# Two groups by seven products in more pairs of a trunk's weight chunks, and the squares of x in two turns

## The chip, the core and the metric

The kernel runs on one core of one Trainium2 chip. The metric is device time of one execution in microseconds (us); the median of three runs is quoted, and the profile is of one execution of its own. The engines are TensorE (PE; PEld is its weight load), VectorE (DVE), ScalarE (ACT), GpSimd (POOL) and SyncE (SP), which here only issues transfers. SPq and POOLq are the queues of SP and POOL.

## What is computed

Two layers of a trunk on x of 256 rows by 2048 columns, in float32. Cut to what matters:

```python
for i in range(2):
    h = rmsnorm(x, norm_mix_g[i])
    glu_in, q, k, v, f_logit, g_conv, g_attn = split(h @ w_in[i])
    y_conv = conformer_conv(glu_in, ...)          # depthwise conv over 31 rows, LayerNorm, swish, @ w_conv_out
    y_attn = forgetting_attention(q, k, v, log_sigmoid(f_logit + b)) @ w_attn_out[i]      # 8 heads of 128
    x = x + (sigmoid(g_conv) * y_conv + sigmoid(g_attn) * y_attn) @ w_out[i]
    gate, up = split(rmsnorm(x, norm_ffn_g[i]) @ w_gate_up[i])                           # 2 x 5632 columns
    x = x + (silu(gate) * up) @ w_down[i]
    x = x + sigmoid(rmsnorm(x, norm_ple_g[i]) @ w_ple_gate[i]) * (p[i] @ w_ple_proj[i])
return rmsnorm(x, final_g)
```

## The kernel before

**Three products for one.** Every weight matrix is read in chunks of 512 output columns, and a chunk in groups of four K tiles of 128 rows (a transfer brings two K tiles, 128x1024). TensorE works on float32r values, so each weight tile is split: `split` (L143, L144) makes a high part `wh` with a copy on ACT and a low part `wl` with a subtraction on DVE; the activations are split in the same way. `Sum.add` (L186 to L188) issues high x high, high x low and low x high, each a matmul of 512 columns. A plain group of two chunks is 4 K tiles x 2 chunks x 2 blocks of 128 rows x 3 = 48 matmuls.

**Seven products.** `fast_chunks` takes a pair of chunks, `w1` and `w2`, and treats the first groups by the seven products of the Strassen-Winograd scheme: two chunks and two halves of the K tiles make a 2x2 block product. Such a group is 7 x 2 K tiles x 3 = 42 matmuls. It needs seven splits where a plain group needs four, and combinations of the raw weights: POOL issues one transfer that adds onto a loaded tile (L278), DVE adds and subtracts (L273, L274; the helpers `add` and `sub` are also used for the sums at the end, from PSUM). The activations' side, eight blocks, is made once per norm group by `Fast` (L360, L366, L375, L376); `Norm(..., fast=n)` makes it for the first n groups of four K tiles. The argument `fast` of `fast_chunks` is the list of these, and `ks` are the first K tiles of the plain groups.

**What sets the order.** A scheduler puts the instructions of each engine in an order, mostly that of the code; every engine then works through its own in that order. Buffers bound how far an engine runs ahead: eight of `raw`, five of `wh` and five of `wl`, four single PSUM banks (`ms`) and two double ones (`mm`). Work beside the products is handed out in steps: `run()` calls the functions that wait in `turns` and one of `tasks` (the attention heads: scores and softmax, transposes, product with v; twelve tasks for four heads); `fill(n)` gives n units of credit to `background`, DVE's depthwise conv and the conv branch's norm. `chunk` does one `run()` and one `fill(7)` for each of its groups. In `fast_chunks` `go()` treats half a plain group; those that are called among the seven products are quiet, the later ones do a `run()` and a `fill` of 3 or 4. What is left is flushed: `while tasks: run()` behind the attention branch's gates, `while background: fill(9)` behind the first pair of the conv branch's gates.

**The stages of a layer, in order:** GLU input, values, keys and queries by `chunk`; the attention branch's gates in two pairs (`sigmoids(GATE_B, 1)` and `sigmoids(GATE_B + 2, 1)`, one group by seven products each); the attention projection in four chunks; the conv branch's gates in two pairs of two groups each, with the conv projection; `wOut`; then gate-and-up in parts of 3, 4 and 4 column chunks, c = 0 to 10, where a pair is the gate chunk and the up chunk of one c, each part followed by two down pairs; then the embeddings' gate in two pairs (n = 0 and 2) with one group each. Pair c = 0 is plain. The others take `FAST[c % 2]` groups: two for even c, one for odd c.

**The beginning of the first layer.** x is read twice, transposed for the first chunk and in rows (`xt`) for the residual and the sums of squares. `late(b)` issues the two halves of `xt` in two turns, each released by a tiny ACT copy (L532, L533); its third turn loads the remaining vectors (L536, L537), takes the squares of all of x (`squares`, L424, eight ACT instructions), finishes the norm and hands over to `early`, which builds the `Fast` blocks.

Of the kernel before, what the change touches and what calls it, by code (L numbers as in the profile page):

```python
# [16 lines left out]
P = 128  # L17
# [11 lines left out]
KD = D // P  # L29
# [5 lines left out]
PAIRS = 28  # L35
WARM = 14
RAWS = 8

FAST = (2, 1)
CONV = 7  # L40
PAUSE = 2 * CONV, lambda: None

# [5 lines left out]
def trunk(ctx, tc, xT, xR, pT, wI, wF, wC, wA, wOut, wGU, wD, wPG, wPP, vec, bF, gF, out):  # L48
    nc = tc.nc
# [31 lines left out]
    turns = deque()  # L81
# [400 lines left out]
    norm = Norm(0)  # L482
# [46 lines left out]
    def late(b):  # L529

        if b < 2:
            act.activation(xt[:, b, :1], recent[0][:, 0, :1], AF.Copy)  # L532
            nc.sync.dma_start(xt[:, b, :], xR[:, b, :])  # L533
            turns.append(lambda: late(b + 1))
            return
        nc.sync.dma_start(vecs[:, KD:], vec[:, KD:])  # L536
        nc.sync.dma_start(bfs, bF.rearrange("l h -> (l h)").partition_broadcast(P))  # L537
        for n in range(N4):
            norm.squares(n)
        norm.finish()  # L540
        turns.append(early)

    for i in range(L):
# [296 lines left out]
        def sigmoids(c, nf):  # L840

            ts = []

            def gate(t):
                for b in range(2):
                    act.activation(t[:, b, :], t[:, b, :], AF.Sigmoid, scale=norm.r(b))  # L846
                ts.append(t)

            gate(fast_chunks(norm.fast[:nf], wI[i, c], wI[i, c + 1], norm.xs, range(4 * nf, KD, 4), gate))
            return ts  # L850
# [1 line left out]
        def gated_by(t, pp):  # L852
            dve.tensor_tensor(t, t, pp, op=ALU.mult)

        y_att = sigmoids(GATE_B, 1) + sigmoids(GATE_B + 2, 1)
        while tasks:
            run()
        for n in range(N4):
# [19 lines left out]
            xc = xt[:, :, n * 512 : (n + 1) * 512]  # L878
            dve.tensor_tensor(xc, xc, acc, op=ALU.add)

        norm = Norm(g_ffn, fast=max(FAST))
        def onto_x(norm, n):
            def go(y):
                residual(n, y)
# [11 lines left out]
            )  # L896


        after = Norm(g_ple, fast=1)
        c0 = 0  # L900
        for part, nch in enumerate(FFN_PARTS):
            hid = {}
            fast_hid = [Fast() for _ in range(nch - 2)]
            for c in range(c0, c0 + nch):
                w1, w2 = wGU[i, 2 * c], wGU[i, 2 * c + 1]
                o = pair() if c == 0 else None

                def gate(g):
                    nonlocal o
                    if o is None:  # L910
                        o = g
                    for b in range(2):
                        act.activation(o[:, b, :], g[:, b, :], AF.Silu, scale=norm.r(b))

                if c == 0:
                    gate(chunk(by_four(w1), norm.xs))
                    up = chunk(by_four(w2), norm.xs)
                else:
                    nf = FAST[c % len(FAST)]
                    up = fast_chunks(norm.fast[:nf], w1, w2, norm.xs, range(4 * nf, KD, 4), gate)  # L920
                for b in range(2):
                    dve.scalar_tensor_tensor(
                        o[:, b, :], up[:, b, :], norm.r(b), o[:, b, :], op0=ALU.mult, op1=ALU.mult
                    )
                turns.append(
                    lambda c=c, o=o, hid=hid, fast=fast_hid[c - c0] if c - c0 < len(fast_hid) else None:
                    operand(hid, 4 * c, lambda b: o[:, b, :], fast)
                )
# [63 lines left out]
        for n in range(0, N4, 2):  # L992
            for m in range(2):
                e.append(pair())
                for b, t in enumerate(chunk([(wPP[i, n + m], range(2))], ps)):
                    act.activation(e[n + m][:, b, :], t, AF.Copy)
            ending = last and n == N4 - 2
            y = fast_chunks(
                norm.fast, wPG[i, n], wPG[i, n + 1], norm.xs, (4, 8, 12), embedded(n),
                by_block=end if ending else None,  # L1000
            )
            if not ending:
                embedded(n + 1)(y)
# [61 lines left out]
```

## Time and profile before

| | |
|---|---|
| median of three runs | 2809.96 us (2809.64 to 2810.13) |
| the profiled execution's own time | 2809.66 us |
| its span in the profile | 2808.0 us |
| granted TensorE clock, mean | 0.999 |
| transfers | 578.96 MB, mean 206 GB/s |

In a row of the costliest groups the columns are line, engine, operation, what it writes and reads (buffer numbers left out), shapes and count; then busy time, mean of one in ns, and the idle time of the engine ahead of it with what ended it. A timeline row is start, length, engine, line, operation, tiles, count, and in brackets idle time and its releaser. The ends of matmuls are modelled, so their rate is read from their starts.

### The profile page before, as it was taken

The page shows a single profiled execution, that of the slowest core. Times are in us where ns is not written, and L with a number is a line of the kernel's source. Part 1 is how long each engine was busy: PE and PEld are TensorE (multiplying, and loading weights), DVE is VectorE, ACT ScalarE, POOL GpSimd, SP SyncE. Part 2 cuts the span into 40 slices and gives each one's busy share as a digit, 9 for nine tenths or more (in the row PEclk, how much of TensorE's full clock was granted, in tenths as well). Part 3 has the DMA queues.
Part 4 walks back from the last instruction along what each step waited for, and adds up shares of the span by engine and source line. Part 5 has one row for each costly group of instructions (what it writes and reads, how often), then busy time and mean ns, then how long its engine had stood idle before and what let it go on. Part 6 is the DMA issues. An engine that isn't in the chain of part 4 may idle for free.

```text
span 2808.0 us, 34895 instructions
## 1 busy us (share of the span) xinstructions
PE 2789.8 (99%) x12640; PEld 2307.2 (82%) x12640; DVE 2429.0 (87%) x2927; ACT 1628.9 (58%) x1962; POOL 68.7 (2%) x109
## 2 busy tenths in 40 slices
PE   9999999999999999999999999999999999999998
PEld 7888888888888888888888888888888888888886
DVE  7998788887989888889869987888789899888897
ACT  7445655565556555656644456555655465555565
POOL 0000000000000000000000000000000000000000
PEclk9999999999999999999999999999999999999999
DMA  8555467665677666676655555666666676676673
GB/s 298 188 184 184 168 191 224 204 214 189 216 226 227 202 224 219 216 222 215 203 173 191 185 168 173 220 213 190 228 192 213 217 230 220 203 233 210 211 247 121
DMA packets 159870, 578.96 MB, mean 206 GB/s; under 512 B 18001, under 2 KB 18257, under 8 KB 159441
## 3 DMA queue, kind: packets, MB, share of 16 engines
q1 hardware_dynamic: 149040, 539.50, 56.0%
q0 software_dynamic: 9792, 35.66, 7.2%
q8 instruction: 99, 1.62, 0.2%
q10 hardware_dynamic: 864, 1.57, 0.2%
q14 instruction: 75, 0.61, 0.1%
HBM read 574.56 MB, written 2.10 MB: 205 GB/s over the span
## 4 chain that ended last, share of the span: by engine, by line
PE 95%; DVE 1%; ACT 1%; DMA 1%; issue 1%; SPq 0%; POOL 0%; POOLq 0%; ACTq 0%
PE mm L186 26%; PE mm L187 26%; PE mm L188 26%; PE ms L186 5%; PE ms L188 5%; PE ms L187 5%; PE ms L336 2%; DMA raw<-in_wI_dram 1%; ACT wh L143 1%; DVE wl L144 1%; PE ms L724 0%; DVE raw L273 0%; PE ms L753 0%; PE ms L743 0%; ACT pair L846 0%
## 5 line engine op out<-in xcount | busy, mean ns | idle before, releaser
L143 ACT ACTIVATE wh<-raw 128x1024 fp32r<-128x1024 f32 x1218 | 1271.2, 1059 | 1057.3 <-PE mm L188 669.6
L144 DVE TENSOR_TENSOR wl<-raw,wh 128x1024 fp32r<-128x1024 f32 x1218 | 1463.9, 1221 | 295.1 <-ACT wh L143 288.2
L186 PE MATMUL mm<-wh,pair 128*128 128x512 f32 x3340 | 1307.7, 392 | 0.7 <-ACT pair L326 0.3
L187 PE MATMUL mm<-wl,pair 128*128 128x512 f32 x3340 | 1301.9, 390 | 1.4 <-DVE wl L144 1.4
L188 PE MATMUL mm<-wh,pair 128*128 128x512 f32 x3340 | 1302.1, 390 | 0.5 <-DVE pair L327 0.5
L188 PEld LDWEIGHTS mm<-wh,pair 128*128 128x128 f32 x3340 | 627.0, 188 | 132.4 <-DVE pair L327 1.3
L187 PEld LDWEIGHTS mm<-wl,pair 128*128 128x128 f32 x3340 | 627.4, 188 | 130.6 <-DVE wl L144 3.0
L186 PEld LDWEIGHTS mm<-wh,pair 128*128 128x128 f32 x3340 | 627.3, 188 | 129.5 <-ACT wh L143 1.5
L186 PE MATMUL ms<-wh,pair 128*128 128x512 f32 x588 | 229.5, 391 | 1.9 <-ACT wh L143 1.9
L188 PE MATMUL ms<-wh,pair 128*128 128x512 f32 x588 | 228.9, 389 | 0.0
L187 PE MATMUL ms<-wl,pair 128*128 128x512 f32 x588 | 228.9, 389 | 0.0
L567 DVE SCALAR_TENSOR_TENSOR pair<-pair,vecs,pair 128x256 f32<-128x256 f32 x480 | 201.8, 480 | 0.0
L273 DVE TENSOR_TENSOR raw<-raw,raw 128x1024 f32<-128x1024 f32 x136 | 166.2, 1222 | 2.3
L186 PEld LDWEIGHTS ms<-wh,pair 128*128 128x128 f32 x588 | 110.4, 188 | 27.2 <-ACT wh L143 3.3
L188 PEld LDWEIGHTS ms<-wh,pair 128*128 128x128 f32 x588 | 110.4, 188 | 23.0
L187 PEld LDWEIGHTS ms<-wl,pair 128*128 128x128 f32 x588 | 110.4, 188 | 22.3
L273 DVE TENSOR_TENSOR pair<-pair,ms 128x512 f32<-128x512 f32 x144 | 94.0, 680 | 0.0
L274 DVE TENSOR_TENSOR raw<-raw,raw 128x1024 f32<-128x1024 f32 x68 | 83.3, 1225 | 2.3
L274 DVE TENSOR_TENSOR pair<-mm,pair 128x1024 f32<-128x1024 f32 (+1 forms) x48 | 58.2, 1212 | 18.1 <-PE mm L188 18.1
L273 DVE TENSOR_TENSOR pair<-pair,mm 128x1024 f32<-128x1024 f32 x48 | 58.4, 1216 | 8.6 <-PE mm L188 8.6
L376 DVE TENSOR_TENSOR pair<-pair,pair 128x1024 fp32r<-128x1024 f32 x48 | 58.1, 1219 | 0.0
L375 ACT ACTIVATE pair<-pair 128x1024 fp32r<-128x1024 f32 x48 | 50.2, 1056 | 2.1 <-DVE pair L366 1.2
(167 smaller groups left out, 1054.7 us busy)
## 6 DMA issues: line engine op xcount, KB each, us to landing
raw<-in_wGU_dram SPq DMA_DIRECT2D x352, 512.0 KB, 4.9
raw<-in_wI_dram SPq DMA_DIRECT2D x287, 512.0 KB, 4.0
raw<-in_wD_dram SPq DMA_DIRECT2D x176, 512.0 KB, 5.0
raw<-in_wOut_dram SPq DMA_DIRECT2D x64, 512.0 KB, 4.9
raw<-in_wPG_dram SPq DMA_DIRECT2D x64, 512.0 KB, 5.0
raw<-in_wA_dram SPq DMA_DIRECT2D x32, 512.0 KB, 4.4
raw<-in_wC_dram SPq DMA_DIRECT2D x32, 512.0 KB, 5.6
raw<-in_wGU_dram POOLq DMA_DIRECT2D x30, 512.0 KB, 8.0
```

Of the source, the lines that this page charges most:

```text
L143: act.activation(h, raw, AF.Copy)
L144: dve.tensor_tensor(l, raw, h.bitcast(F32), op=ALU.subtract)
L186: pe.matmul(self.t, lhsT=xh, rhs=wh, start=start, stop=False)
L187: pe.matmul(self.t, lhsT=xh, rhs=wl, start=False, stop=False)
L188: pe.matmul(self.t, lhsT=xl, rhs=wh, start=False, stop=self.left == 0)
L273: add = lambda o, a, b: dve.tensor_tensor(o, a, b, op=ALU.add)
L274: sub = lambda o, a, b: dve.tensor_tensor(o, a, b, op=ALU.subtract)
L336: pe.transpose(pt[:, kk * S + b * P : kk * S + (b + 1) * P], src(b)[:, c : c + P], ident)
L375: act.activation(h, t, AF.Copy)
L376: dve.tensor_tensor(l, t, h.bitcast(F32), op=ALU.subtract)
L567: dve.scalar_tensor_tensor(cv[c], u[c][:, j : j + S], w, cv[c], op0=ALU.mult, op1=ALU.add,)
```

## The change

```diff
-FAST = (2, 1)
...
-        nc.sync.dma_start(vecs[:, KD:], vec[:, KD:])
-        nc.sync.dma_start(bfs, bF.rearrange("l h -> (l h)").partition_broadcast(P))
+        if b == 2:
+            nc.sync.dma_start(vecs[:, KD:], vec[:, KD:])
+            nc.sync.dma_start(bfs, bF.rearrange("l h -> (l h)").partition_broadcast(P))
         for n in range(N4):
-            norm.squares(n)
+            norm.squares(n, [b - 2])
+        if b == 2:
+            turns.append(lambda: late(3))
+            return
         norm.finish()
         turns.append(early)
...
-        y_att = sigmoids(GATE_B, 1) + sigmoids(GATE_B + 2, 1)
+        y_att = sigmoids(GATE_B, 2) + sigmoids(GATE_B + 2, 2)
...
-        norm = Norm(g_ffn, fast=max(FAST))
+        norm = Norm(g_ffn, fast=2)
...
-        after = Norm(g_ple, fast=1)
+        after = Norm(g_ple, fast=2)
...
-                    nf = FAST[c % len(FAST)]
+                    nf = 1 if c == c0 else 2
...
-                norm.fast, wPG[i, n], wPG[i, n + 1], norm.xs, (4, 8, 12), embedded(n),
+                norm.fast[: 1 + n // 2], wPG[i, n], wPG[i, n + 1], norm.xs, range(4 + 2 * n, KD, 4), embedded(n),
```

In gate-and-up all pairs but the first of a part have two groups by seven products (c = 1, 5 and 9 had one; c0 is the first c of a part: 0, 3, 7). Both pairs of the attention branch's gates have two instead of one, and so has the embeddings' second pair, for which the norm ahead of it now makes two `Fast` groups. The squares of x are taken in two turns, one for each block of 128 rows, and `early` comes a turn later. Line numbers in the new file are two lower up to the diff's first place in `late` and two higher behind it: L144 is L142, L274 is L272, L735 is L737.

In gate-and-up, DVE's rows at pair 5 of the first layer, from the last split of its first group on, before (`raw` and `wl` are weight tiles, `pair` with `ms` the sums from PSUM):

```order
L144 TENSOR_TENSOR wl_7531<-raw_7423,wh_7530 128x1024
L274 TENSOR_TENSOR pair_7414<-pair_7414,ms_7510 128x512
L144 TENSOR_TENSOR wl_7548<-raw_7545,wh_7547 128x1024
L273 TENSOR_TENSOR pair_7415<-pair_7414,ms_7498 128x512
L144 TENSOR_TENSOR wl_7592<-raw_7589,wh_7591 128x1024
L273 TENSOR_TENSOR pair_7414<-pair_7414,ms_7522 128x512
L273 TENSOR_TENSOR pair_7415<-pair_7415,ms_7522 128x512
L144 TENSOR_TENSOR wl_7610<-raw_7607,wh_7609 128x1024
```

and at the end of the second group of the same pair now:

```order
L142 TENSOR_TENSOR wl_7646<-raw_7572,wh_7645 128x1024
L271 TENSOR_TENSOR raw_7572<-raw_7572,raw_7575 128x1024
L272 TENSOR_TENSOR raw_7570<-raw_7572,raw_7570 128x1024
L142 TENSOR_TENSOR wl_7657<-raw_7572,wh_7656 128x1024
L271 TENSOR_TENSOR raw_7577<-raw_7577,raw_7572 128x1024
L142 TENSOR_TENSOR wl_7668<-raw_7570,wh_7667 128x1024
L142 TENSOR_TENSOR wl_7679<-raw_7577,wh_7678 128x1024
L142 TENSOR_TENSOR wl_7699<-raw_7696,wh_7698 128x1024
L272 TENSOR_TENSOR pair_7444<-pair_7444,ms_7540 128x512
L142 TENSOR_TENSOR wl_7743<-raw_7740,wh_7742 128x1024
```

The sums from PSUM (`ms`) stood directly behind the first group; a second group with its combinations of raw weights now stands ahead of them.

At the end of the attention branch's gates, TensorE's rows before, at the product with v (L753, L754) of one of the layer's last heads, with the first of the twelve weight products behind it:

```order
L753 MATMUL ms_2937<-tmp_2869,pair_1371 128x256
L754 MATMUL ms_2937<-tmp_2869,pair_1371 128x128
L186 MATMUL mm_2719<-wh_2948,pair_494 128x512
L187 MATMUL mm_2719<-wl_2949,pair_494 128x512
L188 MATMUL mm_2719<-wh_2948,pair_495 128x512
```

and now, with a head's product with v (L755, L756), the transposes of the next (L745) and the scores of the one behind it (L726, L728, L729) in one row:

```order
L755 MATMUL ms_2991<-tmp_2924,pair_1371 128x256
L756 MATMUL ms_2991<-tmp_2924,pair_1371 128x128
L745 MATMUL ms_3000<-ident,tmp_2949 128x128
L726 MATMUL ms_3007<-pair_2027,pair_2491 128x128
L728 MATMUL ms_3007<-chs_922,nident 128x128
L745 MATMUL ms_3000<-ident,tmp_2949 128x128 x2
L729 MATMUL ms_3007<-chs_922,nident 128x128
L726 MATMUL ms_3017<-pair_2027,pair_2491 128x256
L728 MATMUL ms_3017<-chs_922,nident 128x256
L729 MATMUL ms_3017<-chs_922,nident 128x256
L755 MATMUL ms_3027<-tmp_3004,pair_1371 128x256
L756 MATMUL ms_3027<-tmp_3004,pair_1371 128x128
```

The tasks that were spread among the second pair's products are left for the flush behind it and stand closer together; 26, 10, 19 and 17 weight products lie between the scores and the transposes of the last four heads.

At the beginning, SP's rows with the second half of `xt`, before:

```order
L137 DMA raw_377<-in_wI_dram 128x1024
L533 DMA xt<-in_xR_dram 128x2048
L536 DMA vecs<-in_vec_dram 128x624
L537 DMA bfs<-in_bF_dram 128x16
L137 DMA raw_430<-in_wI_dram 128x1024
```

and now:

```order
L135 DMA raw_377<-in_wI_dram 128x1024
L535 DMA vecs<-in_vec_dram 128x624
L531 DMA xt<-in_xR_dram 128x2048
L536 DMA bfs<-in_bF_dram 128x16
L135 DMA raw_417<-in_wI_dram 128x1024
```

The load of `xt` waits for the tiny ACT copy, which stood ahead of the copy of the first GLU chunk out of PSUM (L595) and now stands behind it; the weight loads behind it on SP wait with it.

## The prediction

> **What bounds the kernel now.** I read the page first: busy time by engine, then the chain that ended last, then the costliest groups.
>
> ```profile
> PE 2789.8 (99%) x12640; PEld 2307.2 (82%) x12640; DVE 2429.0 (87%) x2927; ACT 1628.9 (58%) x1962; POOL 68.7 (2%) x109
> ...
> PE 95%; DVE 1%; ACT 1%; DMA 1%; issue 1%; SPq 0%; POOL 0%; POOLq 0%; ACTq 0%
> ...
> L143 ACT ACTIVATE wh<-raw 128x1024 fp32r<-128x1024 f32 x1218 | 1271.2, 1059 | 1057.3 <-PE mm L188 669.6
> L144 DVE TENSOR_TENSOR wl<-raw,wh 128x1024 fp32r<-128x1024 f32 x1218 | 1463.9, 1221 | 295.1 <-ACT wh L143 288.2
> ...
> L273 DVE TENSOR_TENSOR raw<-raw,raw 128x1024 f32<-128x1024 f32 x136 | 166.2, 1222 | 2.3
> ```
>
> 95% of the chain is TensorE, and ACT's largest wait (669.6 us) is for TensorE to give a buffer back: the copies run ahead until the five buffers of `wh` are full. That alone would make each matmul left out a gain. But DVE is at 87% of the whole and must make a low part for every weight tile, so the second question is where DVE is short. The timelines of DVE and TensorE around pair 5 of the first layer's gate-and-up loop (one group by seven products, between two pairs that have two) give the pace of both.
>
> ```profile
> 872.67 1.22 DVE L144 TENSOR_TENSOR wl<-raw,wh 128x1024 fp32r<-128x1024 f32 x1
> ...
> 880.28 0.39 PE L187 MATMUL ms<-wl,pair 128*128 128x512 f32 x1
> ...
> 893.40 1.22 DVE L144 TENSOR_TENSOR wl<-raw,wh 128x1024 fp32r<-128x1024 f32 x1
> ...
> 895.01 0.39 PE L186 MATMUL mm<-wh,pair 128*128 128x512 f32 x1
> 895.24 0.39 PE L187 MATMUL mm<-wl,pair 128*128 128x512 f32 x1
> ...
> 897.51 0.40 PE L188 MATMUL mm<-wh,pair 128*128 128x512 f32 x1
> ...
> 852.80 4.62 DVE L144 TENSOR_TENSOR wl<-raw,wh 128x1024 fp32r<-128x1024 f32 x4
> ```
>
> The twelve products from 895.01 to 897.51 start (897.51 - 895.01) / 11 = 0.227 us apart: although each row says 0.39, they overlap and nothing waits. On DVE four splits take 4.62 us, so they start (4.62 - 1.22) / 3 = 1.13 us apart. The low part made from 872.67 to 873.89 is used at 880.28: DVE leads by 6.39 us when this pair begins. The one made from 893.40 to 894.62 is used at 895.24: the lead has sunk to 0.62 us at the end of the group by seven products, because such a group wants ten DVE instructions for 9.5 us of products. **The lead is what can be spent**; below zero TensorE idles.
>
> **The products saved.** The sums by window are cut at the first product of the pairs 4, 5, 6 and of the first down pair behind them (columns: length, then busy time and count of PE, PEld, DVE, ACT, POOL; the clock; DMA share; GB/s).
>
> ```profile
> 838.33:880.05 41.72, 41.72 (x189) 34.62 (x188) 41.23 (x42) 27.42 (x29) 0.86 (x1) 1.00 0.65 209
> 880.05:923.14 43.09, 43.09 (x195) 35.74 (x194) 36.18 (x37) 24.30 (x26) 1.70 (x2) 1.00 0.71 219
> 923.14:964.87 41.73, 41.73 (x190) 34.62 (x188) 39.76 (x38) 25.52 (x27) 0.85 (x1) 1.00 0.70 226
> 964.87:1007.96 43.09, 43.09 (x196) 35.74 (x195) 34.35 (x33) 21.20 (x22) 1.70 (x2) 1.00 0.71 218
> ```
>
> A pair with one group takes 43.09, with two 41.73: a converted group is worth 1.36 us, which is six products of 0.227 (48 become 42). Per layer the change converts three groups in gate-and-up (pairs 1, 5, 9), two in the attention branch's gates (one in each pair) and one in the embeddings' second pair; 6 in a layer, 12 in all: 12 x 1.36 = **-16.4 us**, 72 products. The order of instructions has exactly 72 products fewer, so that the change might not do what it says is excluded.
>
> **What each converted group adds.** Three more splits (L143 and L144) and three combinations (two at L273, one at L274), which last as long as a split (1222 ns beside 1221): six DVE instructions, 6 x 1.13 = 6.8 us of DVE; 3.2 us of ACT, which is 58% busy and waits for TensorE most; and one more accumulating transfer on POOL's queue (SP issues four loads either way).
>
> ```profile
> raw<-in_wGU_dram SPq DMA_DIRECT2D x352, 512.0 KB, 4.9
> ...
> raw<-in_wGU_dram POOLq DMA_DIRECT2D x30, 512.0 KB, 8.0
> ```
>
> That transfer follows its own load: 4.9 + 8.0 = 12.9 us from issue to use. Eight buffers of `raw` are fetched ahead, some 8 x 1.13 = 9 us of DVE beside the lead of 6.39, so it is hidden, as for the second groups that exist; I take 0, and cost it at up to 1 us in each converted pair if DVE's lead is gone.
>
> **Gate-and-up.** In the three windows from 838.33 to 964.87 DVE is busy 41.23 + 36.18 + 39.76 = 117.2 us of 126.5. Now 124.0 of 125.2: full, but not over. Pair 5 starts with the lead that it has today, 6.39, and passes its first group with the rows of today, so 0.62 stays. The second group follows at once, without the five additions behind the first: ten DVE instructions and two plain splits are 13.6 us beside 9.5 + 5.4 = 15.0 us of products, so the lead grows by 1.4. Pair 6, which today starts with a full lead, then starts as pair 5 does, or lower by what DVE loses to waits of its own. Bounds of TensorE's wait there: 0 (124.0 fits) and 1.2 us (if pair 6 gets none of the 1.2 left); I take 0.5, near the fitting end, for pairs 6 and 10 in both layers: **+2 us**. The pace of 1.13 is that of the row of four splits in 4.62 us, and a rule speaks against it: the Trainium skill ("VectorE: DVE Perf Modes", The DRAIN you can't avoid) says that the next Vector operation does not start until the pipe behind the last one is empty. By that each split would keep DVE for its 1.22, and the sum would be the 2830 worked out in the first rival; by the row it is the 2795 below. That row disagrees with the rule for splits that stand back to back.
>
> Pairs 1 and 2 follow plain chunks whose DVE is half idle, and the down pair behind them has DVE to spare: 0, at most 0.5 in a layer. In the embeddings' second pair the second norm group exists already as plain tiles; its four differences and two splits replace four smaller low parts, inside the first pair: 0, bounds -1 and +1.
>
> **The attention branch's gates.** Here the change moves more than it adds. With two groups the part that calls waiting tasks shrinks from ten steps to four in each pair, so eight of the 24 attention tasks (most of the last four heads' work) are left for the loop behind the second pair, and the conv branch's norm is pushed back by 2 x 21 = 42 units of credit, from the second gate pair into the attention projection and the first conv gate pair.
>
> ```profile
> 295.49:343.90 48.41, 47.48 (x216) 38.72 (x215) 39.71 (x62) 34.20 (x50) 0.00 (x0) 1.00 0.57 194
> ...
> 306.19 0.39 PE L188 MATMUL ms<-wh,pair 128*128 128x512 f32 x1
> 306.75 0.50 PE L186 MATMUL ms<-wh,pair 128*128 128x512 f32 x1 [0.17 <-ACT wh L143]
> 308.01 0.50 PE L186 MATMUL ms<-wh,pair 128*128 128x512 f32 x1 [0.75 <-ACT wh L143]
> ...
> 276.59 0.38 PE L724 MATMUL ms<-pair,pair 128*128 128x128 f32 x2
> ...
> 280.84 0.30 PE L743 MATMUL ms<-ident,tmp 128*128 128x128 f32 x1 [0.20 <-DVE tmp L737]
> ```
>
> In the second gate pair TensorE waits today, inside the seven products: starts 0.56 and 1.26 us apart instead of 0.227 lose 1.4 us, because two heads' softmax sits on DVE ahead of the splits. That work moves behind the group: -1.4 in each layer, bounds 0 and -2.2 (all steps of that group). Against it: a head takes 4.25 us from its first score product (276.59) to its first transpose (280.84), and TensorE takes its instructions in order. In the new order 26, 10, 19 and 17 weight products stand between the scores and the transposes of the last four heads: 5.9, 2.3, 4.3 and 3.9 us, and the 10 are joined by another head's product and score, some 1.5 us. That leaves about 0.5 us for the second head, 0.4 for the fourth: I take +1 in each layer, bounds 0 and 8 (each of four heads short by 4.25 - 2.3). Then the first conv gate pair:
>
> ```profile
> 388.50:429.30 40.80, 40.80 (x182) 33.78 (x181) 37.84 (x34) 24.99 (x25) 0.00 (x0) 1.00 0.67 220
> ...
> 378.96 1.23 DVE L144 TENSOR_TENSOR wl<-raw,wh 128x1024 fp32r<-128x1024 f32 x1
> ...
> 388.72 0.39 PE L187 MATMUL ms<-wl,pair 128*128 128x512 f32 x1
> ```
>
> It has 3.0 us of DVE free and receives, by the order, the last part of the conv norm, about 30 instructions of 128x256; at an estimated 0.33 us each (a quarter of a split's elements, between a quarter and a half of its 1.13) that is 10 us, so DVE falls back 7 us over the pair. It starts with a lead of 388.72 - 380.19 = 8.5, of which a group needs 6.39 - 0.62 = 5.8: 2.7 are spare, and half of the 7 come behind the groups, where products outlast splits. I take +0.4, bounds 0 and 4.3 (all 7 ahead of the dip). Net for both layers: 2 x (-1.4 + 1 + 0.4) = **0**.
>
> **Squares of x.** Today seven squares stand in a row on ACT, and behind them the copy whose low part TensorE waits for.
>
> ```profile
> 35.84 0.61 ACT L424 ACTIVATE tmp<-xt 128x512 f32<-128x512 f32 x1
> ...
> 42.84 0.50 PE L187 MATMUL mm<-wl,pair 128*128 128x512 f32 x1 [1.10 <-DVE wl L144]
> ...
> 28.43 0.33 SPq L533 DMA_DIRECT2D xt<-in_xR_dram  x1
> ...
> 30.32 1.03 ACT L595 ACTIVATE pair<-mm 128x1024 f32<-128x1024 f32 x1 [1.92 <-PE mm L188]
> ```
>
> Four squares need the first half of x only, and now run earlier: 3 x 0.61 = 1.8 us could go. But the load of the second half, issued at 28.43, now stands behind the copy of 30.32 (its release is moved past it on ACT): about 3 us later, and every load behind it on SP's queue too. The four squares then wait for it. I take **-0.3**, bounds -1.6 (the wait at 42.84 gone) and +1.5 (the load late by 3 instead).
>
> **Sum**, from the profiled execution's 2809.66: -16.4 + 2 + 0 - 0.3 = 2795.0; the median of the runs, 2809.96, lies 0.30 above, so **2795** us.
>
> **Rivals.** *DVE becomes the bound in gate-and-up.* For: 124.0 of 125.2 leaves nothing, and pair 5 today sinks to 0.62. Against: the flat stretch runs at 1.13. Over pairs 4 to 6 DVE has 42 + 37 + 38 + 6 = 123 instructions, so each 0.01 us of pace is 1.2 us; the first 1.2 us are free by the sum above, and 0.6 by the lead. At 1.16 it falls 3.7 back and TensorE waits some 2 to 3 us at each of four places: about 12 in all, 2807. At the full 1.22 it falls 11 back, 9 of them waited for: 36 in all, 2830, with slower than before reached at about 1.18. That last case is the one of the Trainium skill's rule.
>
> *The flushed heads are exposed*, the case on the other side. If the weight products between do not get their splits in time (the order puts up to four splits on DVE inside a head's softmax), TensorE waits for whole chains behind the second gate pair: 4 heads x 4.25 us x 2 layers = 34 less the 2 counted: 2827. It turns slower than before by more than 0.2% (5.6 us, about what a measurement of this kernel can tell from no change) from (15 + 5.6 + 2) / 8 = 2.8 us a head. Against: today's heads wait 0.2 us. Half-exposed heads give about 2807 again.
>
> *Nothing waits*: without the +2 and with -2.2 and no new wait at the gates, 2809.66 - 16.4 - 4.4 - 0.3 = 2788.6, or 2789.
>
> **How the numbers follow.** Forecast (2791 to 2800) 0.60; DVE at 1.16 or half-exposed heads (2800 to 2815, about 2807) 0.23, some 0.10 of it still below 2804.3; heads exposed or DVE at its full rows (over 2815) 0.05; nothing waits (below 2791) 0.12. Faster by over 0.2% (below 2804.3): 0.60 + 0.12 + 0.10 = 0.82; within: 0.13; slower: 0.05. The range, 2789 to 2804, leaves out a little of the last case below and the 0.13 and 0.05 above, together about 0.2: its lower end is the sum with nothing waiting, its upper end lies three quarters of the way from the forecast to the 2807 of the middle cases.
>
> **What would show it.** Pairs 1, 5 and 9 at 41.7 in the sums by window, and pairs 6 and 10 still at 41.7 (42.2 with my wait); the first low part of pair 6 some 6 us ahead of its product, as pair 5's today. The two gate pairs and the attention projection up to the first conv gates together 2.7 us shorter, TensorE's waits there moved from L186 behind L143 to the transposes (L745 in the new file) behind L739. Waits of TensorE for L142 of over 1 us in pairs 5, 6, 9 or 10 would make the DVE rival right; waits of over 2 us for each of the last heads the other one. Wrong altogether it would be if products started more than 0.227 us apart throughout.

## The result, and the profile after

The changed kernel takes **2793.0 us** (median of four runs, 2792.8 to 2793.7) beside 2809.8 before: ratio 0.994, 95% interval 0.9927 to 0.9953. The forecast was 2795, range 2789 to 2804. The profiled execution took 2793.7 us, its span is 2791.8, and the span of before is 2808.0: 16.2 us to account for.

The page of the kernel after, busy time by engine, the chain that ended last, and the costliest groups that answer to those shown of before:

```profile
PE 2773.9 (99%) x12568; PEld 2293.5 (82%) x12568; DVE 2507.1 (90%) x3003; ACT 1660.0 (59%) x2002; POOL 79.4 (3%) x121
...
PE 93%; DVE 3%; issue 3%; ACT 1%; POOL 0%; POOLq 0%; ACTq 0%; DVEq 0%
...
L141 ACT ACTIVATE wh<-raw 128x1024 fp32r<-128x1024 f32 x1254 | 1300.5, 1058 | 1022.7 <-PE mm L186 576.7
L142 DVE TENSOR_TENSOR wl<-raw,wh 128x1024 fp32r<-128x1024 f32 x1254 | 1501.0, 1219 | 212.4 <-ACT wh L141 204.9
```

There are 72 matmuls fewer (12640 to 12568) and 36 splits more (1218 to 1254). VectorE went from 87% to 90%, its idle time ahead of splits from 295 to 212 us; TensorE still holds 93% of the chain (95% before). The sums by window of the kernel after, cut at the first product of the gate-and-up pairs 4, 5, 6 and of the down pair behind them (columns as in the prediction):

```profile
832.55:874.28 41.73, 41.73 (x190) 34.62 (x188) 41.24 (x42) 27.41 (x29) 1.70 (x2) 1.00 0.64 204
874.28:916.00 41.72, 41.72 (x189) 34.61 (x188) 41.43 (x42) 27.13 (x29) 1.25 (x2) 1.00 0.72 226
916.00:957.77 41.77, 41.77 (x189) 34.54 (x188) 41.06 (x40) 24.99 (x27) 1.30 (x2) 1.00 0.76 231
957.77:1000.86 43.09, 43.09 (x196) 35.74 (x194) 34.35 (x33) 21.23 (x22) 1.70 (x2) 1.00 0.72 226
```

Pair 5 went from 43.09 to 41.72; pair 6 became 0.04 longer (0.08 in the second layer). VectorE is busy 123.7 of 125.2 us, where the prediction had 124.0. Its lead in pair 6 is in the timeline of the kernel after:

```profile
908.03 2.35 DVE L142 TENSOR_TENSOR wl<-raw,wh 128x1024 fp32r<-128x1024 f32 x2
...
916.23 0.39 PE L185 MATMUL ms<-wl,pair 128*128 128x512 f32 x1
...
926.85 2.52 DVE L142 TENSOR_TENSOR wl<-raw,wh 128x1024 fp32r<-128x1024 f32 x2
...
928.51 0.39 PE L185 MATMUL ms<-wl,pair 128*128 128x512 f32 x1
```

The second split of the first row ends at 910.38 and is used at 916.23: the pair begins 5.85 us ahead. The first of the row at 926.85 ends 1.22 us later, at 928.07, and is used at 928.51: 0.44 us is the smallest lead of the pair. Nothing waits, but little is left.

The table gives stages from first product to first product, in us, both layers together; "forecast" is the prediction's term with the products of that stage in it.

| stage | before | after | measured | forecast |
|---|---|---|---|---|
| gate-and-up, pairs 1 to 10 | 844.5 | 836.6 | -7.9 | -8.2 + 2 = -6.2 |
| attention: gates, projection, first conv gates | 370.4 | 362.6 | -7.7 | -5.5 + 0 = -5.5 |
| embeddings, with the next layer's first GLU product or the end | 231.8 | 231.6 | -0.2 | -2.7 |
| first two GLU products of layer 0 | 47.4 | 47.0 | -0.4 | -0.3 |
| all | | | -16.2 | -14.7 |

The total hides two errors that nearly cancel: 3.9 us better in the first two rows, 2.5 worse in the third.

### The profile page after: what moved, and what is told of

It reads as the page before. It is cut to its first block, busy times and chain, and to the rows that moved or that the text cites. A ratio compares the mean times of both kernels' runs of the same rounds, so it can differ in the third digit from the quotient of the medians.

```text
span 2791.8 us, 34941 instructions
## 1 busy us (share of the span) xinstructions
PE 2773.9 (99%) x12568; PEld 2293.5 (82%) x12568; DVE 2507.1 (90%) x3003; ACT 1660.0 (59%) x2002; POOL 79.4 (3%) x121
## 4 chain that ended last, share of the span: by engine, by line
PE 93%; DVE 3%; issue 3%; ACT 1%; POOL 0%; POOLq 0%; ACTq 0%; DVEq 0%
PE mm L186 25%; PE mm L185 25%; PE mm L184 25%; PE ms L184 5%; PE ms L185 5%; PE ms L186 5%; PE ms L334 2%; DVE wl L142 1%; DVE raw L271 0%; PE ms L726 0%; ACT wh L141 0%; PE ms L755 0%; DVE pair L374 0%; PE ms L745 0%; DVE pair L271 0%
## 5 line engine op out<-in xcount | busy, mean ns | idle before, releaser
L141 ACT ACTIVATE wh<-raw 128x1024 fp32r<-128x1024 f32 x1254 | 1300.5, 1058 | 1022.7 <-PE mm L186 576.7
L142 DVE TENSOR_TENSOR wl<-raw,wh 128x1024 fp32r<-128x1024 f32 x1254 | 1501.0, 1219 | 212.4 <-ACT wh L141 204.9
L184 PE MATMUL mm<-wh,pair 128*128 128x512 f32 x3224 | 1261.9, 392 | 1.1 <-ACT pair L324 0.7
L185 PE MATMUL mm<-wl,pair 128*128 128x512 f32 x3224 | 1256.6, 390 | 0.9 <-DVE wl L142 0.8
L186 PE MATMUL mm<-wh,pair 128*128 128x512 f32 x3224 | 1256.8, 390 | 0.5 <-DVE pair L325 0.5
L186 PEld LDWEIGHTS mm<-wh,pair 128*128 128x128 f32 x3224 | 605.2, 188 | 128.4 <-DVE pair L325 1.4
L185 PEld LDWEIGHTS mm<-wl,pair 128*128 128x128 f32 x3224 | 605.6, 188 | 126.3 <-DVE wl L142 3.2
L184 PEld LDWEIGHTS mm<-wh,pair 128*128 128x128 f32 x3224 | 605.4, 188 | 126.0 <-ACT pair L324 1.7
L184 PE MATMUL ms<-wh,pair 128*128 128x512 f32 x680 | 265.7, 391 | 0.1
L186 PE MATMUL ms<-wh,pair 128*128 128x512 f32 x680 | 264.7, 389 | 0.0
L185 PE MATMUL ms<-wl,pair 128*128 128x512 f32 x680 | 264.6, 389 | 0.0
L271 DVE TENSOR_TENSOR raw<-raw,raw 128x1024 f32<-128x1024 f32 x160 | 195.4, 1222 | 2.6
L184 PEld LDWEIGHTS ms<-wh,pair 128*128 128x128 f32 x680 | 127.7, 188 | 28.0 <-ACT pair L998 0.9
L186 PEld LDWEIGHTS ms<-wh,pair 128*128 128x128 f32 x680 | 127.6, 188 | 26.7
L272 DVE TENSOR_TENSOR raw<-raw,raw 128x1024 f32<-128x1024 f32 x80 | 98.0, 1225 | 2.6
L271 DVE TENSOR_TENSOR pair<-pair,ms 128x512 f32<-128x512 f32 x144 | 93.9, 680 | 0.0
L272 DVE TENSOR_TENSOR pair<-mm,pair 128x1024 f32<-128x1024 f32 (+1 forms) x48 | 58.1, 1210 | 11.5 <-PE mm L186 11.4
L271 DVE TENSOR_TENSOR pair<-pair,mm 128x1024 f32<-128x1024 f32 x48 | 58.3, 1215 | 5.5 <-PE mm L186 5.5
L374 DVE TENSOR_TENSOR pair<-pair,pair 128x1024 fp32r<-128x1024 f32 x52 | 62.8, 1217 | 0.0
```

Source lines behind the costliest of these rows:

```text
L141: act.activation(h, raw, AF.Copy)
L142: dve.tensor_tensor(l, raw, h.bitcast(F32), op=ALU.subtract)
L184: pe.matmul(self.t, lhsT=xh, rhs=wh, start=start, stop=False)
L185: pe.matmul(self.t, lhsT=xh, rhs=wl, start=False, stop=False)
L186: pe.matmul(self.t, lhsT=xl, rhs=wh, start=False, stop=self.left == 0)
L271: add = lambda o, a, b: dve.tensor_tensor(o, a, b, op=ALU.add)
```

## Experiments

All are timed against the kernel before in the same session (its median 2809.6 to 2809.9). Ratios carry 95% intervals of 0.09% to 0.17% to either side (2.5 to 4.6 us), so smaller differences, and those against the changed kernel, are read from the lengths of the stages in the traces.

**The four parts alone.** First the rule of the gate-and-up pairs, on the kernel before:

```diff
-                    nf = FAST[c % len(FAST)]
+                    nf = 1 if c == c0 else 2
```

> The kernel before with the new rule of the gate-and-up pairs alone (one group in the first pair of a part, two in all others; 6 more groups of seven products). Theory (products removed, VectorE ahead all the way): 6 x 1.36 = -8.2 us, less about 0.2 for short waits in pairs 6 and 10, so -8.0 (2801.8 us). Rival (VectorE is what bounds pairs 5, 6, 9 and 10 at 1.13 us per operation, as the prediction took with +0.5 for each of pairs 6 and 10): -6 us. Nothing but the gate-and-up pairs may move.

Measured 2802.6 us, ratio 0.9974 (0.9964 to 0.9984): -7.0. Each of the six converted pairs takes 41.73 for 43.09; pairs 6 and 10 take 41.80 to 41.83 where they took 41.73. By the stages that is -8.16 + 0.33 = -7.83 in gate-and-up, of which the last down pair of the first layer gives 0.15 back; the rest of the difference to -7.0 lies mostly in the time up to the second GLU product, which differs by up to 1.2 us from run to run. The pairs themselves settle it: short waits of 0.1 us, and no VectorE bound here.

Then the attention branch's gates alone:

```diff
-        y_att = sigmoids(GATE_B, 1) + sigmoids(GATE_B + 2, 1)
+        y_att = sigmoids(GATE_B, 2) + sigmoids(GATE_B + 2, 2)
```

> The kernel before with two groups in both pairs of the attention branch's gates alone (4 more groups). Theory (besides 4 x 1.36 = 5.5 us of products, TensorE loses waits in these pairs, because fewer steps of the attention heads run in them; after's trace puts that at 1.0 to 1.2 us a layer): -7.7 us (2802.1). Rival A (products alone, as the prediction had it): -5.5 us. Rival B (the heads' last steps, run with no products beside them, leave TensorE waiting 2.8 us a head or more): above 0.

Measured 2802.06, ratio 0.9972 (0.9962 to 0.9983): -7.6, the theory's number. The stages from the gates to the first conv gates are those of the changed kernel to within 0.25 us a layer.

The embeddings alone:

```diff
-        after = Norm(g_ple, fast=1)
+        after = Norm(g_ple, fast=2)
...
-                norm.fast, wPG[i, n], wPG[i, n + 1], norm.xs, (4, 8, 12), embedded(n),
+                norm.fast[: 1 + n // 2], wPG[i, n], wPG[i, n + 1], norm.xs, range(4 + 2 * n, KD, 4), embedded(n),
```

> The kernel before with the second group in the embeddings' gate alone (2 more groups, and the second group made in the norm ahead of it). Theory (the seven products' sums of the second group stand in VectorE's queue ahead of the last residual, so the transposes of x come late, about +1.1 us a layer, and the kernel's tail grows by 0.8): -0.2 us (2809.6). Rival (only the products change, what after's trace shows there came from the other edits): -2.7 us (2807.1).

Measured 2809.73, ratio 1.000 (0.9991 to 1.0009): +0.1. Twelve products fewer gained nothing. The second product with the projected embeddings takes 4.50 for 3.61 us in both layers, as in the changed kernel, so that loss belongs to this edit.

The squares alone:

```diff
         for n in range(N4):
-            norm.squares(n)
+            norm.squares(n, [b - 2])
+        if b == 2:
+            turns.append(lambda: late(3))
+            return
```

> The kernel before with the squares of x in two turns alone. Theory: -0.4 us (2809.4), all of it in the first two products of layer 0 (0.5 longer and 1.0 shorter). Rival (the second load of x comes later and holds something up, or nothing moves): 0 to +1.5 us. With five rounds 0.4 us may be within the interval; the stage's length in the trace decides.

Measured 2808.65, ratio 0.9996 (0.9987 to 1.0005): -1.0, inside the interval. In the trace the second GLU product takes 22.5 us for 23.5, as in every run that has this edit (22.5 to 22.9) and in no other (23.5); the first one varies between 23.0 and 24.4 with and without it. So about -1.0 is the edit's, the 0.5 by which the first product seemed longer is not.

The four parts add up to -7.0 - 7.6 + 0.1 - 1.0 = -15.5 beside the -16.8 of all together: the 1.3 between them lies within the intervals, so they are nearly independent as far as these runs can tell.

**Why the gates gave more than their products.** On the kernel before, a pair keeps one group, but `fast_chunks` calls no waiting task until the last four splits are left:

```diff
-        state["quiet"] = False
+        state["quiet"] = hush is not None
         go(len(left) - 2 * len(ks))
         add(u1, u1, c1())
         first(u1)
+        if hush is not None:
+            go(len(left) - hush)
+            state["quiet"] = False
...
-        y_att = sigmoids(GATE_B, 1) + sigmoids(GATE_B + 2, 1)
+        y_att = sigmoids(GATE_B, 1, 4) + sigmoids(GATE_B + 2, 1, 4)
```

> The kernel before, with one group in the attention branch's gates as it was, but the steps of the attention heads run only behind the last four splits of a pair, as they do in a pair with two groups. No product is saved. Theory (of the 3.8 us that a layer gained there, 1.1 came from steps of the heads that no longer stand between the products): -2.2 us (2807.6). Rival (the gain beyond the products needs the shorter list of products, or VectorE's other order): 0 (2809.8). Against both: the heads' last steps alone cost more than they free, above 2811.

Measured 2807.42, ratio 0.9991 (0.9982 to 1.0000): -2.5. The sums by window over the same four stages (first gate pair, second, attention projection, first conv gate pair) of layer 0, first of the kernel before:

```profile
244.10:295.49 51.39, 51.19 (x251) 42.63 (x250) 40.17 (x62) 32.45 (x48) 0.86 (x1) 1.00 0.52 174
...
sum 185.20, PE 184.07 PEld 151.91 DVE 152.48 ACT 117.26 POOL 3.49; mean PE 46.02 PEld 37.98 DVE 38.12 ACT 29.32 POOL 0.87
```

then of this run:

```profile
244.75:290.72 45.97, 45.97 (x216) 38.28 (x215) 32.47 (x37) 28.41 (x36) 0.86 (x1) 1.00 0.60 195
...
sum 183.75, PE 183.75 PEld 151.64 DVE 147.57 ACT 116.16 POOL 3.29; mean PE 45.94 PEld 37.91 DVE 36.89 ACT 29.04 POOL 0.82
```

and of the kernel after:

```profile
243.61:288.22 44.61, 44.61 (x210) 37.16 (x209) 38.95 (x43) 31.48 (x39) 1.70 (x2) 1.00 0.63 198
288.22:335.05 46.83, 46.64 (x221) 38.81 (x220) 44.06 (x59) 32.90 (x43) 0.00 (x0) 1.00 0.68 227
335.05:383.88 48.83, 48.82 (x225) 39.88 (x224) 36.17 (x67) 28.34 (x45) 2.43 (x3) 1.00 0.52 162
383.88:424.84 40.96, 40.96 (x182) 33.73 (x180) 40.96 (x53) 29.21 (x39) 0.00 (x0) 1.00 0.59 193
```

The interval of this run reaches up to no change, so the stages decide. Before, 1.1 of the 185.2 us have no TensorE work in them; in the hushed run none, although it does every product, and the four stages are 1.5 us shorter in each layer. The kernel after needs 181.2: 2.7 less for its twelve products and 1.2 less beside them. The theory holds: what is moved away from the seven products is worth 1.2 to 1.5 us a layer without a single product saved. While a pair is quiet it calls neither the heads' tasks nor the conv work, so the run moves both and doesn't tell them apart.

The trace shows the way by which a head gets in. ScalarE's rows behind the first gate pair, in the kernel before:

```profile
297.73 1.28 ACT L735 ACT_TABLE_LOAD   x1
...
300.03 1.28 ACT L846 ACT_TABLE_LOAD   x1
...
301.96 1.04 ACT L143 ACTIVATE wh<-raw 128x1024 fp32r<-128x1024 f32 x1
```

and in the hushed run:

```profile
293.05 1.34 ACT L849 ACTIVATE pair<-pair,rt 128x512 f32<-128x512 f32 x2
```

A head's exponentials (L735) stood between the two halves of the gate's sigmoid (L846), and ScalarE loaded its table of functions twice more, 1.28 us each. The copy of the weights behind them (L143) began 6.5 us after the second pair's first product; in the hushed run the two halves stand in one row (L849), and it begins 3.6 us after (294.29 beside 290.72).

**Where the embeddings' gain went.** VectorE and TensorE's weight loads in the kernel after, at the end of the last down pair of layer 0:

```profile
1289.47 0.75 DVE L364 TENSOR_TENSOR pair<-pair 128x256 f32<-128x256 f32 x2
1290.14 0.41 DVE L364 TENSOR_TENSOR pair<-pair,pair 128x256 f32<-128x256 f32 x1
...
1293.08 1.22 DVE L374 TENSOR_TENSOR pair<-pair,pair 128x1024 fp32r<-128x1024 f32 x1
...
1295.36 1.22 DVE L374 TENSOR_TENSOR pair<-pair,pair 128x1024 fp32r<-128x1024 f32 x1
...
1299.19 1.21 DVE L881 TENSOR_TENSOR xt<-xt,pair 128x1024 f32<-128x1024 f32 x1
...
1300.46 0.86 PEld L334 LDWEIGHTS ms<-ident,xt 128*128 128x128 f32 x8 [0.77 <-DVE xt L881]
```

The second group's differences (L364) and low halves (L374) stand ahead of the last residual (L881). It ends at 1300.40, and eight transposes of `xt` wait 0.77 us for it, with all products behind them. If that is the cause, the part of the work that only the seven products need can come later:

```diff
-            sub(M1, B11, B12, ALU.subtract)
...
+        def rest(self):
+            self.sums()
+            self.halved(self.f[1])
+            self.f = None
...
         if n == N4 - 1:
             norm.finish()
+            turns.extend(f.rest for f in norm.fast if f.later)
...
-        after = Norm(g_ple, fast=2)
+        after = Norm(g_ple, fast=2)
+        after.fast[1].later = True
```

(`sums` holds the four differences, `halved` the copy and the low part of one tile; `make` does only the first tile at once where `later` is set.)

> The changed kernel, with the second embedding group's four sums and the halves of them (four VectorE operations of 128x256, one of 128x1024, one ScalarE copy) issued behind the last transposes of x instead of ahead of them. Theory (these operations make the last residual late, and with it TensorE's transposes): the second product with the projected embeddings goes back from 4.50 to about 3.6 us in both layers, and the first gate pair by up to 0.2: 2791.0 us, -1.8 to -2.2 against the changed kernel. Rival (the transposes wait for something else, such as the residual's own input): no change, 2793.0, and 4.5 us as before.

Measured 2790.2, ratio 0.993 (0.9915 to 0.9945): -2.8 against the changed kernel. VectorE in this run:

```profile
1298.25 1.22 DVE L896 TENSOR_TENSOR xt<-xt,pair 128x1024 f32<-128x1024 f32 x1
...
1301.14 0.42 DVE L379 TENSOR_TENSOR pair<-pair 128x256 f32<-128x256 f32 x1
```

The residual (L896 here) now ends at 1299.47 and the first difference (L379) comes behind it. The second product with the projected embeddings is back at 3.7 us in both layers, and the gate pair behind it is 0.5 shorter, where up to 0.2 was expected: that is why the gain is larger than the theory's 1.8 to 2.2. The rival is out.

The rest of the loss is in the kernel's tail, whose second group is taken away again here:

```diff
-        after = Norm(g_ple, fast=2)
+        after = Norm(g_ple, fast=1 if i == L - 1 else 2)
...
+            nf = 1 if last else 1 + n // 2
             y = fast_chunks(
-                norm.fast[: 1 + n // 2], wPG[i, n], wPG[i, n + 1], norm.xs, range(4 + 2 * n, KD, 4), embedded(n),
+                norm.fast[: nf], wPG[i, n], wPG[i, n + 1], norm.xs, range(4 * nf, KD, 4), embedded(n),
```

> The changed kernel, with one group again in both pairs of the last layer's embeddings' gate. Theory (in the last layer the second group costs 1.1 us of waits ahead of the gate and 0.8 us of tail for its 1.4 us of products, so it loses 0.6 there): 2792.4 us, with the last 110 us of the kernel 0.6 us shorter than the changed kernel's. Rival (it is worth its products wherever it stands): 2794.4.

Measured 2792.69, ratio 0.9938 (0.9924 to 0.9953), 0.3 below the changed kernel and within its noise. The stages agree with the theory: the last layer's embeddings take 0.9 and 0.2 us less up to the last pair, and that pair to the end takes 54.24 for 53.70, together 0.6 less. The tail itself, VectorE in the kernel after:

```profile
2774.22 1.82 DVE L965 TENSOR_TENSOR pair<-pair,pair 128x1024 f32<-128x1024 f32 x2
...
2779.19 0.68 DVE L272 TENSOR_TENSOR pair<-ms,pair 128x512 f32<-128x512 f32 x1
...
2781.82 0.88 DVE L988 TENSOR_SCALAR xt<-xt,rt 128x512 f32<-128x512 f32 x2 [0.47 <-POOL rt L448]
2782.62 0.68 DVE L966 TENSOR_TENSOR xt<-xt,pair 128x512 f32<-128x512 f32 x1
```

and in the kernel before:

```profile
2796.61 0.68 DVE L274 TENSOR_TENSOR pair<-ms,pair 128x512 f32<-128x512 f32 x1
...
2799.06 0.69 DVE L964 TENSOR_TENSOR xt<-xt,pair 128x512 f32<-128x512 f32 x1
```

With two groups no plain split is left between the third output of the gate and the fourth, so both embeddings reach VectorE together (one row at L965, x2). The last block's difference (L272) to its addition (L966) is 3.43 us, with the scaling of the other block (L988) in between; before it was 2.45. The six products saved are worth 1.36 and the last stretch is only 0.56 shorter (54.26 to 53.70): 0.8 us of tail, and these rows show where it arises.

**How much VectorE still has.** The changed kernel, with no pair left at one group:

```diff
-                    nf = 1 if c == c0 else 2
+                    nf = 2
```

> The changed kernel, with two groups also in the first gate-and-up pair of the second and third parts (4 more groups of seven products). Theory (VectorE's split of weights still ends ahead of its product; the smallest lead in the changed kernel is 0.4 us, in pair 6, and each converted pair takes about 0.5 of it, so short waits come in pairs 6 and 10): 4 x 1.36 = -5.4, +1 of waits, 2788.6 us. Rival (VectorE is the bound from four converted pairs in a row on: each then lasts as long as its VectorE work, 124 us for three, and what is gained in pairs 3 and 7 is given back in pairs 4 to 6 and 8 to 10): 2792 to 2793, TensorE's waits for the split at 4 us or more in all.

Measured 2788.2, ratio 0.9923 (0.9906 to 0.9939): -4.8. Its sums by window, pairs 3 and 7 of layer 0 and, last, pair 10:

```profile
790.33:831.13 40.80, 40.80 (x181) 33.78 (x180) 38.47 (x35) 24.75 (x25) 1.15 (x2) 1.00 0.75 229
1040.28:1081.08 40.80, 40.80 (x181) 33.78 (x180) 38.47 (x35) 24.74 (x25) 1.53 (x3) 1.00 0.78 240
1164.53:1206.62 42.09, 42.00 (x189) 34.53 (x188) 41.36 (x40) 24.97 (x27) 1.16 (x2) 1.00 0.76 230
```

Pairs 3 and 7 go from 42.16 to 40.80. Pair 10, the fourth in a row, pays 0.3 in the first layer and 0.1 in the second. VectorE is full there, and still not the bound.

**A third group, to make VectorE the bound.**

```diff
-        norm = Norm(g_ffn, fast=2)
+        norm = Norm(g_ffn, fast=3)
...
-                    nf = 1 if c == c0 else 2
+                    nf = 1 if c == c0 else 3 if c > 7 else 2
```

> The changed kernel, with a third group made in the norm and three groups of seven products in gate-and-up pairs 8, 9 and 10 of both layers. This asks what the prediction left as a rival: what VectorE's pace is where it is the bound. By its 1.13 us per operation a pair is 41.3 + 6.8 = 48.1 us of VectorE work beside 40.4 of products; three pairs 144.4 against 121.1, of which a lead of about 7 us absorbs some: 3 pairs take about 137 us for 125.2 in the changed kernel, +12 a layer, 2817 us (the third group's own sums may add 1 to 3). Rival pace 1.16 (operations spread by waits): +4 a layer more, 2825. Rival pace 1.22 (each operation starts when the one before it has ended, the length of one operation in the trace): 52.0 a pair, +24 a layer, 2841. Rival (VectorE never becomes the bound): 2785.

Measured 2834.8, ratio 1.0089 (1.0074 to 1.0105): +25 against before, +42 against the changed kernel. Pairs 8, 9, 10 and the down pair of this run, then short windows at the border of the last two:

```profile
1083.00:1122.50 39.50, 39.50 (x175) 32.56 (x174) 38.89 (x35) 24.55 (x25) 1.73 (x2) 1.00 0.69 203
1122.50:1168.50 46.00, 41.66 (x175) 32.03 (x175) 45.65 (x44) 26.75 (x29) 2.54 (x3) 1.00 0.75 220
1168.50:1221.30 52.80, 45.74 (x199) 35.69 (x198) 52.32 (x54) 32.81 (x38) 2.56 (x3) 0.97 0.71 207
1221.30:1273.20 51.90, 49.48 (x202) 38.93 (x203) 45.82 (x49) 28.55 (x37) 1.70 (x2) 0.90 0.61 191
...
1216.60:1221.30 4.70, 0.01 (x1) 0.00 (x0) 4.70 (x9) 3.92 (x6) 0.00 (x0) 1.00 0.07 31
1221.30:1225.80 4.50, 2.92 (x11) 2.10 (x11) 4.50 (x7) 1.99 (x3) 0.00 (x0) 0.53 0.01 4
...
1228.00:1232.00 4.00, 3.89 (x10) 2.92 (x10) 3.57 (x6) 3.00 (x5) 0.00 (x0) 0.53 0.37 131
1232.00:1236.00 4.00, 4.00 (x20) 3.27 (x19) 3.96 (x5) 0.60 (x1) 0.00 (x0) 1.00 0.09 19
```

VectorE is the bound in pairs 9 and 10 (45.65 of 46.0, 52.32 of 52.8): in pair 9 TensorE waits 4.3 us for the halves of weights, 3.9 of it for ScalarE's copies (L141), and those wait most for VectorE's combinations (L271). The three pairs take 138.3 us. The theory had 137; the pace of 1.22, with at least 149, is out. Between 1.13 and 1.16 this run doesn't decide, because the edit does more than was meant: three groups use up every plain split inside the groups, so no task is called in these pairs (175 matmuls in pairs 8 and 9, products alone, where the changed kernel has 189 or 190 with the transposes), and the transposes of the hidden values pile up ahead of the down pair. There TensorE stands still for 4.7 us, until VectorE has made their low part (L374); this wait lies at the end of pair 10. Behind it TensorE runs at a granted clock of 0.50 to 0.53 for some ten. With 1.6 and 0.6 us more of waits that is the down pair's 51.9 us for 44.0, which no theory had: 2 x (13.1 + 7.9) = 42.

**Putting together what gained.** The changed kernel with the later sums and two groups in all pairs:

```diff
-                    nf = 1 if c == c0 else 2
+                    nf = 2
...
+            turns.extend(f.rest for f in norm.fast if f.later)
...
+        after.fast[1].later = True
```

> The changed kernel with the edits of two runs together: the second embedding group's sums behind the last transposes of x, and two groups in every gate-and-up pair but the first. Theory (they lie in different stages, so their gains of 2.8 and 4.8 us add up): 2785.4 us. Rival (VectorE has no room for both, or one edit's gain was the other's): 2787 or more.

Measured **2785.0**, ratio 0.9911 (0.9898 to 0.9925): 24.8 us below the kernel before and 8.0 below the changed one, the sum of the two gains (7.6) and a little. It is the best version of this study.

And on top of it the embeddings' first pair:

```diff
-                norm.fast[: 1 + n // 2], wPG[i, n], wPG[i, n + 1], norm.xs, range(4 + 2 * n, KD, 4), embedded(n),
+                norm.fast, wPG[i, n], wPG[i, n + 1], norm.xs, (8, 12), embedded(n),
```

> The run with both edits, and two groups also in the first pair of the embeddings' gate of both layers (2 more groups). Theory (the second group's sums end before its first product, some 10 us after the pair begins): 2 x 1.36 = -2.7 us, 2782.7. Rival (TensorE waits there for the sums, since they are made in that pair's first microseconds): 0 or worse, 2785.4 or more, and the pair no shorter than 43.2 us.

Measured 2789.13, ratio 0.9925 (0.9912 to 0.9937): 4 us slower than without it (the profiled execution, at 2787.4 the fastest of five, 2.4 slower). That is the rival's side, but not its mechanism. The pair itself is shorter by 1.4 in both layers, as the theory says; but in layer 0 the product with the projected embeddings behind it takes 8.3 us for 2.7. TensorE's waits there, in this run:

```profile
PE ms L334 <- DVE xt L982: 1.8, 1, 1.8
PE mm L184 <- ACT wh L141: 1.5, 1, 1.5
```

and two products behind them:

```profile
1349.90 0.63 PE L184 MATMUL mm<-wh,pair 128*128 128x512 f32 x1
1350.33 0.63 PE L185 MATMUL mm<-wl,pair 128*128 128x512 f32 x1
```

The waits are 3.2 of the 5.6 us. Behind them the products start 0.43 us apart, with a granted clock of 0.55 from 1349.2 to 1353.0; that and eight transposes are the rest. Fewer plain splits mean fewer calls of tasks in the pair, so the next norm's transposes and the sums of its two groups come together behind it: the same displacement as at the attention gates, here onto a stage of 2.7 us that can't cover it. The last layer, whose next norm has no such groups, keeps its 2.7; no run takes the displacement alone away. In the last layer the gain goes into the tail again (+1.4).

## Why the prediction was right, and where it was not

**Products: right.** Every converted group gave six products: 1.36 us in pairs 1, 5 and 9 of both layers. VectorE's and POOL's additions were hidden, as taken.

**Gate-and-up, +2 taken, +0.2 found.** The mechanism was right (pair 6 begins 5.85 us ahead, nearly as pair 5 did with 6.39, and sinks to 0.44) but it doesn't go below zero. The step that was mis-sized is "I take 0.5" for pairs 6 and 10: the room of 1.2 us in three pairs is nearly enough for VectorE, those pairs are 0.04 to 0.08 us longer, and the whole kernel has waits of TensorE for the split of 0.8 us, 0.5 of it in the second GLU product (list of waits of the kernel after):

```profile
PE mm L185 <- DVE wl L142: 0.8, 3, 0.5
PE ms L334 <- DVE xt L881: 0.7, 2, 0.4
...
PE ms L745 <- DVE tmp L739: 0.4, 2, 0.2
```

With four pairs in a row the dip does come, at 0.3 and 0.1 us. The rival of a VectorE bound failed at two groups and holds at three. The rule that the prediction weighed, of the Trainium skill ("VectorE: DVE Perf Modes", The DRAIN you can't avoid), does not fit these splits as the prediction took it: in the kernel after, two splits of 1.22 us take 2.35 in the row at 908.03, so they start 1.13 apart; three groups would have cost 149 us by it and cost 138. The same section of the Trainium skill adds a limit, which the prediction left out: an operation that is not held starts earlier.

**Attention gates, 0 taken beside the products, -2.2 found.** All three parts were seen and all three mis-sized, and the place of the first was wrong: the prediction had two heads' softmax "on DVE ahead of the splits", but VectorE stood idle there (2.4 us before the split at 303.03), and it was ScalarE that the head held up. Recovered waits: in the two gate pairs, starts further apart than 0.227 fell from 2.9 to 0.4 us in layer 0, where -1.4 was taken (bound -2.2, for the second pair alone). Flushed heads: +1 taken; the row at L745 shows 0.2 a layer, and the attention projection gained 0.7 us of such gaps in layer 0. First conv gate pair: +0.4 taken, +0.16 found; its smallest lead fell from 2.6 to 0.8 us. Gaps went down by 1.8 in layer 0 and the stages by 1.2 more than the products; the 0.5 between them lies around TensorE's other work, and was not taken apart. The hushed run shows that the displacement alone makes this gain: its gaps between products are those of the changed kernel to within 0.2 us. The rival on the other side (2.8 us a head) is out.

**Embeddings, 0 taken beside the products, +2.5 found.** This is the step that failed: the second group's "four differences and two splits replace four smaller low parts, inside the first pair: 0, bounds -1 and +1". They come ahead of that pair, before the last residual, and stop the transposes: 0.9 us in the product with the projected embeddings and 0.2 in the gate pair, in each layer. With the tail's 0.8 that is 3.0; 0.5 comes back in the first layer's second pair (1.7 shorter for 1.4 of products) and in the GLU product behind it. What the order of a single engine does to the last link before a stage's transposes was not asked. The tail's 0.8 was not considered either. The run with the sums behind the transposes shows the first part; the stages of the two tails show the second.

**Squares, -0.3 taken, about -1.0 found.** TensorE's wait at the split fell from 1.10 to 0.51 us (0.44 with this edit alone), which is 0.6 of it; the other 0.4 was not taken apart. The load that was feared showed no cost in this stage.

That the total of 2795 came out within 2 us is partly luck, because 3.9 us better and 2.5 worse nearly cancel; the sign and most of the size rest on the products, which were safe.

## What to carry to other kernels

Work that is deferred out of a tight stretch can gain more than the arithmetic that is saved there, if the stretch that takes it up has room, and lose more if that stretch is short: look at where each deferred call lands before counting what it frees. When a new operand is prepared ahead of a stage, prepare only what the first products need and put the rest behind the last link that the stage waits for. A lead that sinks to 0.4 us cost under 0.1 us here; count waits below zero, not fullness.

## What the runs showed of the hardware

A wait of TensorE can cost twice. In the run with three groups the wait of 4.7 us was followed by about ten at a granted clock of 0.50 to 0.53, products 0.43 us apart in place of 0.227. The Trainium skill ("TensorE: Matmul & The Clock Gate", What's actually happening) has half the clock after an idle window of about 3.4 us; this wait agrees. The same run also shows the lower clock without such a wait, at 1174 to 1177 us, behind waits of 1.15, 0.15 and 0.63 us close together, in a timeline of TensorE:

```profile
1171.84 0.50 PE L184 MATMUL ms<-wh,pair 128*128 128x512 f32 x1 [1.15 <-ACT wh L141]
...
1174.45 0.63 PE L186 MATMUL mm<-wh,pair 128*128 128x512 f32 x1
1174.88 0.63 PE L184 MATMUL mm<-wh,pair 128*128 128x512 f32 x1
```

The run with the first embedding pair shows it too, behind waits of 1.5 and 1.8 us, so a single long gap is not needed. Nor is a length of wait enough to tell: in the run with three groups one wait of 2.3 us (until 1126.7) left the clock at 1.00, and so did waits of 1.15, 0.63 and 1.04 us close together in its second layer (2578 to 2585).
